# A nineteenth tile for experts' weights, and a pair's sum ahead of the next down products

## The chip, the core and the metric

The kernel runs on one core of a Trainium2 chip. The metric is the time of one execution on the device in microseconds (us). Engines are named as in the profile: PE is TensorE's matmuls, PEld its weight loads, DVE is VectorE, ACT is ScalarE, POOL is GpSimd, SP is SyncE, whose queue issues the DMAs.

## What is computed

256 tokens of width 1024 go through two blocks in float32. The first block mixes tokens (a gated spatial product and a recurrent mixer), then sends every token to 2 of 32 experts and adds their weighted outputs. The second block has two layers of attention, each with a large MLP. The change lies in the experts' stage:

```python
def expert_block(args):
    tok_b, e = args
    xb = xpad[tok_b]
    h = jax.nn.silu(xb @ w_gate[e]) * (xb @ w_up[e])
    return h @ w_down[e]
```

An expert has w_gate and w_up of 1024 x 512 and w_down of 512 x 1024, all float32, 6 MiB together. The 32 experts have 192 MiB, and every one of them is computed.

## The kernel before

**Experts.** A token is given one of 64 slots of its expert. `gather` (L1361) makes the input of four experts at a time, `xg`, by one-hot matrices. For each expert `gate_up` (L1421) multiplies the 64 slots with both matrices, 64 recorded matmuls `gups`, and ScalarE and VectorE make the hidden state `h`. `down_proj` (L1452) calls `hidden_T` (L1444), which transposes `h` on TensorE (`htps`) and lets ScalarE copy it to `hT`; then 16 recorded matmuls `dps` give the outputs. VectorE copies the first 512 columns to the buffer `ysb` of a pair of experts (L1470), ScalarE the other 512 (L1471). `combine` (L1473) multiplies a finished pair with the tokens' weights and adds it into four PSUM banks, 16 recorded matmuls `sums`; the first 8 read what VectorE copied, the other 8 what ScalarE copied. `ysb` has two buffers in the pool `px`.

**The loop** (L1513) is staggered: at step e it asks for gate and up of expert e, then for the down products of expert e-1, and at odd e from 3 on, last, for the sum of the pair (e-3, e-2).

**Weights.** Each matrix is loaded as two tiles of 1 MiB (128 partitions x 8 KB) through SP's queue. The tiles come from three pools: `ring` with 8, `ahead` with 6, `more` with `MORE` = 3, which stands where the mixers' pools stood, and the fourteenth load borrows one buffer of `xg` from `px` once (`BORROW` = 13). So 18 tiles are asked for ahead of the loop, in nine parts of two; afterwards 17 are used in turn. In the order of the loads an expert's gate and up stand ahead of the down matrix of the expert before. A load waits until the last reader of its tile is done. The last 14 tiles but for the borrowed one were used by the loads of the mixers' stage; `px` and `more` start where the pool `split` of the mixers was.

**Order.** The kernel is written with the Tile framework, with `schedule_with_timeline_sim=True`: a planner simulates the program while it is built and fixes each engine's order of instructions. Where the program text names one thing ahead of another, this says which is asked for first, not which is issued first. On the chip the order of each engine is fixed, and semaphores hold an instruction until its inputs are there.

**The branch.** `past_slots` (L1284) holds a slow path for experts with more than 64 tokens. All engines pass the branch at L1287. Its weight tiles `ow` are 2 KB wide, two buffers in the pool `pe`.

Of the kernel before, what the change touches and what calls it, by code (L numbers as in the profile page):

```python
# [13 lines left out]
F32 = mybir.dt.float32  # L14
# [11 lines left out]
P = 128  # L26
T = 256
TX = T + 2
D = 1024
# [5 lines left out]
RING = 8  # L35
SMALL = 4
AHEAD = 6
MORE = 3
BORROW = 13
WAIT = 5  # L40
IDLE = 8
# [3 lines left out]
def block_kernel(ctx: ExitStack, tc: tile.TileContext, A: dict, out: bass.AP):  # L45

    nc = tc.nc
# [73 lines left out]
    loaded = []  # L121
# [529 lines left out]
    with tc.tile_pool(name="pa", bufs=1, reuse_waits="tile") as pa:  # L651
# [129 lines left out]
        for i in range(2):  # L781
            v = f[:, 2 * i : 2 * i + 2, :]
# [18 lines left out]
        for i in range(2):  # L801
            v = sc((P, 2, T), name="qs")
# [290 lines left out]
    with (  # L1093
# [56 lines left out]
        for m in range(2):  # L1150
            v = lgm[:, m].rearrange("p g e -> p (g e)")
# [91 lines left out]
        wg_all, wu_all, wd_all = A["w_gate"][0], A["w_up"][0], A["w_down"][0]  # L1243
        tiles = {}
        rings = [next(source[0]) for _ in range(RING + AHEAD)]
# [4 lines left out]
        def load_next(v, c):  # L1250
            pool = next(rings)
            return load(v, c, pool, "xg" if pool is px else "w")

        source[0] = itertools.repeat(ring)

        def load_expert(e, part):

            if part == "d" and e == NE - 1:
                tiles[e, part] = []
                for i in (0, 512):  # L1260
                    t = next(rings).tile([P, 2048], F32, tag="w", name="w").rearrange("p (k c) -> p k c", c=512)
                    for j in range(2):
                        v = wd_all[e, j * 256 : (j + 1) * 256, i : i + 512].rearrange("(p k) c -> p k c", k=2)
                        loaded.append(nc.sync.dma_start(t[:, 2 * j : 2 * j + 2, :], v))
                    tiles[e, part].append(t)
            elif part == "d":
                tiles[e, part] = [
                    load_next(wd_all[e, i : i + 256, :].rearrange("(p k) c -> p k c", k=2), D) for i in (0, 256)
                ]
            else:  # L1270
                w = wg_all if part == "g" else wu_all
                tiles[e, part] = [
                    load_next(w[e, i : i + 512, :].rearrange("(p k) c -> p k c", k=4), 512) for i in (0, 512)
                ]

        order = []
        for e in range(NE):
            order += [(e, "g"), (e, "u")] + ([(e - 1, "d")] if e else [])
        order.append((NE - 1, "d"))
        nxt = (RING + AHEAD + MORE + 1) // 2  # L1280
        for o in order[:nxt]:
            load_expert(*o)

        def past_slots():  # L1284

            rv = nc.values_load(rint[0:1, 0:1], min_val=0, max_val=T)
            with tc.If(rv > SLOTS):  # L1287
                rb2 = mm(name="rbps")
                spread(r2, rb2[:, 0:T])
                n2T = [sc((P, 2, T), name="n2T") for _ in range(4)]  # L1290
                for k in range(KD):
                    nc.vector.scalar_tensor_tensor(
                        n2T[k // 2][:, k % 2, :],
                        res[:, k, :],
                        col("n2", k, 1),
                        rb2[:, 0:T],
                        op0=ALU.mult,
                        op1=ALU.mult,
                    )
                over = bt("over", (P, 2, NE))  # L1300
                nc.vector.tensor_scalar(over, rank, SLOTS + 0.5, None, op0=ALU.is_ge)
                nc.vector.tensor_tensor(over, over, wt, op=ALU.mult)
                with tc.For_i(0, NE, 1) as ei:
                    wps = mm(name="owps")
                    for m in range(2):
                        nc.tensor.matmul(
                            wps[:, m * P : (m + 1) * P],
                            over[:, m, 0:1].to_broadcast([P, P]),
                            ident,
                            start=True,  # L1310
                            stop=True,
                        )
                    wrow = pe.tile([P, T], F32, tag="hw", name="wrow", bufs=1)
                    nc.vector.tensor_copy(wrow, wps[:, 0:T])

                    def weights(src):
                        w = pe.tile([P, 512], F32, tag="ow", name="ow")
                        w = w.rearrange("p (k c) -> p k c", c=src.shape[2])
                        nc.sync.dma_start(w, src.rearrange("e (k p) c -> p (e k) c", p=P))
                        return w  # L1320

                    for f in range(4):
                        gp = mm((P, 2, T), name="ogp")
                        for s, src in enumerate((wg_all, wu_all)):
                            for k0 in (0, 4):
                                w = weights(src[ds(ei, 1), k0 * P : (k0 + 4) * P, f * P : (f + 1) * P])
                                for k in range(4):
                                    nc.tensor.matmul(
                                        gp[:, s, :],
                                        w[:, k, :],  # L1330
                                        n2T[(k0 + k) // 2][:, k % 2, :],
                                        start=(k0 + k == 0),
                                        stop=(k0 + k == KD - 1),
                                    )
                        o = small.tile([P, T], F32, tag="nf", name="oh", bufs=3)
                        nc.scalar.activation(o, gp[:, 0, :], AF.Silu)
                        nc.vector.tensor_tensor(o, o, gp[:, 1, :], op=ALU.mult)
                        nc.vector.tensor_tensor(o, o, wrow, op=ALU.mult)
                        for c in range(2):
                            w = weights(wd_all[ds(ei, 1), f * P : (f + 1) * P, c * 512 : (c + 1) * 512])  # L1340
                            for pr in range(2):
                                dp = mm((P, 2, T), name="odp")
                                for i in range(2):
                                    k = 2 * pr + i
                                    nc.tensor.matmul(
                                        dp[:, i, :], w[:, 0, k * P : (k + 1) * P], o, start=True, stop=True
                                    )
                                v = res[:, 4 * c + 2 * pr : 4 * c + 2 * pr + 2, :]
                                nc.vector.tensor_tensor(v, v, dp, op=ALU.add)
                    shifted = bt("shifted", (P, 2, NE))  # L1350
                    nc.vector.tensor_copy(shifted[:, :, 0 : NE - 1], over[:, :, 1:NE])
                    nc.vector.tensor_copy(over[:, :, 0 : NE - 1], shifted[:, :, 0 : NE - 1])
# [99 lines left out]
        def down_proj(e, h):  # L1452
            hT = hidden_T(h)
            dt = tiles.pop((e, "d"))
            dps = mm(name="dps")
            for f in range(4):
                j, c = f // 2, f % 2
                for half in range(2):
                    nc.tensor.matmul(  # L1459
                        dps[half * 64 : (half + 1) * 64, :],  # L1460
                        hT[:, c, j * 64 : (j + 1) * 64],
                        dt[f // 2][:, f % 2, half * 512 : (half + 1) * 512],
                        start=(f == 0),
                        stop=(f == 3),
                    )
            e2 = e % 2
            if e2 == 0:
                ysb[e // 2] = px.tile([P, D], F32, tag="ysb", name="ysb")
            t = ysb[e // 2]
            nc.vector.tensor_copy(t[e2 * 64 : e2 * 64 + 64, 0:512], dps[0:64, :])  # L1470
            nc.scalar.copy(t[e2 * 64 : e2 * 64 + 64, 512:1024], dps[64:128, :])  # L1471
# [40 lines left out]
        prev = None  # L1512
        for e in range(NE + 1):  # L1513
            if e < NE:
                while nxt < len(order) and (e, "u") not in tiles:
                    load_expert(*order[nxt])
                    nxt += 1
                h, silu, prod = gate_up(e)
                if e == 0:
                    weigh(0, hot0)  # L1520
                if e % 4 == 2 and e // 4 + 1 < NE // 4:
                    weigh(e // 4 + 1, gather(e // 4 + 1))
            if e:
                if (e - 1, "d") not in tiles:
                    load_expert(*order[nxt])
                    nxt += 1
                if e < NE:
                    down_proj(e - 1, prev)
                if e >= 3 and e % 2 == 1:
                    combine((e - 3) // 2)  # L1530
            prev = h
            if e == 8:
                with ExitStack() as es:
# [832 lines left out]
```

## Time and profile before

| | us |
|---|---|
| median of 3 runs | 1307.55 (1306.39 to 1308.12) |
| the profiled execution | 1305.86 |
| its span, first to last instruction | 1304.2 |
| PE busy | 1260.6 (97%) |
| DVE busy | 651.8 (50%) |
| ACT busy | 511.8 (39%) |

The granted TensorE clock is 0.99 of full speed over the span. The experts' stage goes from about 147 us (first gate matmul) to about 606 us (last sum). The profile's matmuls are pipelined, so the time between two starts says more than one matmul's duration. A float32 matmul is recorded as two.

### The profile page before, as it was taken

What the parts mean: (1) busy time and instruction counts of PE and PEld (TensorE: products, weight loads), DVE (VectorE), ACT (ScalarE), POOL (GpSimd) and SP (SyncE); (2) the same over time, 40 slices, a digit from 0 to 9 for tenths busy, and PEclk for the clock granted to TensorE, in tenths of its full rate; (3) what the DMA queues carried; (4) which work ended last, traced back from release to release, by engine and by line L of the source; (5) the groups of instructions that cost most, each with busy time, mean ns of one, the idle gap of its engine ahead of it and who ended that gap; (6) DMA issues with size and microseconds to landing.
All of it is one profiled execution on the core that took longest, in us unless ns stands there. A gap on an engine that the chain in (4) does not pass through costs nothing.

```text
span 1304.2 us, 22821 instructions
## 1 busy us (share of the span) xinstructions
PE 1260.6 (97%) x9471; PEld 998.6 (77%) x9471; DVE 651.8 (50%) x1268; ACT 511.8 (39%) x918; POOL 65.2 (5%) x92
## 2 busy tenths in 40 slices
PE   8999899999999999999998999999999999999998
PEld 7779565665555556556885679999997879999998
DVE  6765310130101111004776777698667787655554
ACT  7743211111101111113455656544544564654644
POOL 1010000000000000000410000000001120000000
PEclk9999899999999999998998999999999999999999
DMA  7997799999999999998554845599677532555510
GB/s 252 363 411 300 289 421 420 421 421 421 421 420 420 421 421 421 420 415 305 167 195 153 328 164 199 182 353 338 249 272 271 178 130 77 180 172 187 194 66 33
DMA packets 99157, 373.98 MB, mean 287 GB/s; under 512 B 10649, under 2 KB 14442, under 8 KB 74730
## 3 DMA queue, kind: packets, MB, share of 16 engines
q1 hardware_dynamic: 99050, 372.49, 75.1%
q8 instruction: 76, 1.25, 0.4%
q14 instruction: 31, 0.25, 0.1%
HBM read 371.41 MB, written 1.05 MB: 286 GB/s over the span
## 4 chain that ended last, share of the span: by engine, by line
PE 74%; issue 11%; DVE 2%; ACT 1%; POOL 0%; DVEq 0%; ACTq 0%; POOLq 0%
PE hp L448 14%; PE mlp L491 14%; PE gups L1429 13%; PE dps L1459 6%; PE dps L469 5%; PE sums L1477 3%; PE gps L1383 2%; PE oearly L584 2%; PE qp L469 2%; PE olate L491 2%; PE adaps L187 1%; PE kv L469 1%; PE opair L2119 1%; PE kcv L469 1%; PE ptps L2110 1%
## 5 line engine op out<-in xcount | busy, mean ns | idle before, releaser
L152 DVE TENSOR_TENSOR wlo<-w,whi 128x1024 fp32r<-128x1024 f32 (+1 forms) x222 | 269.7, 1218 | 160.9 <-ACT whi L151 158.6
L151 ACT CAST whi<-w 128x1024 fp32r<-128x1024 f32 (+1 forms) x222 | 230.5, 1043 | 251.0 <-PE hp L448 105.6
L1429 PE MATMUL gups<-w,xg 128*64 128x256 f32 x2048 | 236.2, 384 | 3.5 <-PEq L1287 3.5
L1429 PEld LDWEIGHTS gups<-w,xg 128*64 128x64 f32 x2048 | 145.6, 138 | 91.6 <-issue 22.6
L491 PE MATMUL mlp<-hid,whi 128*128 128x256 f32 x1024 | 184.0, 282 | 0.0
L491 PEld LDWEIGHTS mlp<-hid,whi 128*128 128x128 f32 x1024 | 157.2, 188 | 0.4 <-issue 0.4
L491 PE MATMUL mlp<-hid,wlo 128*128 128x256 f32 x512 | 144.8, 283 | 0.0
L448 PE MATMUL hp<-hT_lo,whi 128*128 128x258 f32 x512 | 144.0, 282 | 0.0
L448 PE MATMUL hp<-hT_hi,whi 128*128 128x258 f32 x512 | 143.7, 283 | 0.0
L448 PE MATMUL hp<-hT_hi,wlo 128*128 128x258 f32 x512 | 142.5, 282 | 0.0
L1441 DVE TENSOR_TENSOR h<-h,gups 128x256 f32<-128x256 f32 x32 | 13.5, 421 | 235.8 <-ACT h L1440 235.8
L1459 PE MATMUL dps<-w,hT 128*64 128x512 f32 x496 | 112.7, 596 | 5.1 <-ACT hT L1449 5.1
L491 PEld LDWEIGHTS mlp<-hid,wlo 128*128 128x128 f32 x512 | 96.4, 188 | 1.6 <-issue 1.6
L448 PEld LDWEIGHTS hp<-hT_lo,whi 128*128 128x128 f32 x512 | 96.7, 189 | 0.0
L448 PEld LDWEIGHTS hp<-hT_hi,whi 128*128 128x128 f32 x512 | 96.2, 188 | 0.0
L448 PEld LDWEIGHTS hp<-hT_hi,wlo 128*128 128x128 f32 x512 | 95.9, 189 | 0.0
L1440 ACT ACTIVATE h<-gups 128x256 f32<-128x256 f32 x32 | 12.3, 385 | 183.6 <-PE gups L1429 183.6
L1459 PEld LDWEIGHTS dps<-w,hT 128*64 128x64 f32 x496 | 34.1, 137 | 64.3 <-issue 53.0
L1470 DVE COPY ysb<-dps 64x512 f32<-64x512 f32 x31 | 21.2, 683 | 107.0 <-PE dps L1459 107.0
L1471 ACT COPY ysb<-dps 64x512 f32<-64x512 f32 x31 | 18.0, 582 | 139.0 <-DVE ysb L1470 139.0
L1477 PE MATMUL sums<-sw,ysb 128*128 128x256 f32 x256 | 61.3, 385 | 6.3 <-DVE ysb L1470 6.3
L1477 PEld LDWEIGHTS sums<-sw,ysb 128*128 128x128 f32 x256 | 46.4, 190 | 20.0 <-DVE ysb L1470 13.3
(539 smaller groups left out, 2014.5 us busy)
## 6 DMA issues: line engine op xcount, KB each, us to landing
w<-in_w_gate_dram SPq DMA_DIRECT2D x64, 1024.0 KB
w<-in_w_up_dram SPq DMA_DIRECT2D x64, 1024.0 KB
w<-in_w_down_dram SPq DMA_DIRECT2D x62, 1024.0 KB
w<-in_w_ada_dram SPq DMA_DIRECT2D x48, 1024.0 KB
w<-in_w_mlp_in_dram SPq DMA_DIRECT2D x32, 1024.0 KB
w<-in_w_mlp_out_dram SPq DMA_DIRECT2D x32, 1024.0 KB
w<-in_diff_w_in_dram SPq DMA_DIRECT2D x12, 1024.0 KB
w<-in_w_in_dram SPq DMA_DIRECT2D x10, 1024.0 KB
```

The lines of the kernel that those rows point to most:

```text
L151: nc.scalar.copy(hi, v)
L152: nc.vector.tensor_tensor(lo, v, hi.bitcast(F32), op=ALU.subtract)
L448: nc.tensor.matmul(outs[h], a[:, kk, h * P : (h + 1) * P], b[:, k, :], start=(k == 0 and i == 0), stop=(k == KD - 1 and i == 2),)
L469: nc.tensor.matmul(outs[m], b[:, k, m * P : (m + 1) * P], a[:, kk, :], start=(k == 0 and i == 0), stop=(k == KD - 1 and i == 2),)
L491: nc.tensor.matmul(outs[dc // 2][:, dc % 2, :], a[:, 0, dc * P : (dc + 1) * P], b[:, a0 + kk, :], start=(first and kk == 0 and i == 0 and ...
L584: nc.tensor.matmul(banks[h // 2][:, h % 2, :], a[:, kk, h * P : (h + 1) * P], b[:, k, :], start=(k == 0 and i == 0 and h % 2 == 0), stop=( ...
L1383: nc.tensor.matmul(ps[:, j, :], part[:, m, k * P : (k + 1) * P], hot[:, m].rearrange("p e s -> p (e s)"), start=(n == 0), stop=(n == 3),)
L1429: nc.tensor.matmul(ps[j * 64 : (j + 1) * 64, s * 256 : (s + 1) * 256], xg[:, k, s0 : s0 + SLOTS], w[k // 4][:, k % 4, j * 256 : (j + 1) * ...
L1459: nc.tensor.matmul(dps[half * 64 : (half + 1) * 64, :], hT[:, c, j * 64 : (j + 1) * 64], dt[f // 2][:, f % 2, half * 512 : (half + 1) * 51 ...
L1470: nc.vector.tensor_copy(t[e2 * 64 : e2 * 64 + 64, 0:512], dps[0:64, :])
L1471: nc.scalar.copy(t[e2 * 64 : e2 * 64 + 64, 512:1024], dps[64:128, :])
L1477: nc.tensor.matmul(sums[k // 2][:, k % 2, :], t[:, k * P : (k + 1) * P], sw, start=(pr == 0 and k % 2 == 0), stop=(after is not None and k ...
```

## The change

`MORE` becomes 4, so that 19 tiles are asked for ahead of the loop and 18 are used in turn. The room of 8 KB per partition comes from two places: `ysb` has one buffer instead of two (4 KB), and the branch's tiles `ow` (2 x 2 KB) use that buffer. As the number of tiles ahead is odd, loads are asked for tile by tile instead of in pairs (`load_expert` has an argument `i`, and `load_until` loads until both tiles of a part are there). With one output buffer, the sum of a pair must be asked for ahead of the next pair's first output, so `combine` moves ahead of `down_proj`.

```diff
-MORE = 3
+MORE = 4
...
-        nxt = (RING + AHEAD + MORE + 1) // 2
-        for o in order[:nxt]:
-            load_expert(*o)
+        order = iter([(*o, i) for o in order for i in range(2)])
+
+        def load_until(*o):
+            while len(tiles.get(o, ())) < 2:
+                load_expert(*next(order))
+
+        for _ in range(RING + AHEAD + MORE + 1):
+            load_expert(*next(order))
...
-                        w = pe.tile([P, 512], F32, tag="ow", name="ow")
+                        w = px.tile([P, D], F32, tag="ysb", name="ow", bufs=1)[:, 0:512]
...
-                ysb[e // 2] = px.tile([P, D], F32, tag="ysb", name="ysb")
+                ysb[e // 2] = px.tile([P, D], F32, tag="ysb", name="ysb", bufs=1)
...
-                while nxt < len(order) and (e, "u") not in tiles:
-                    load_expert(*order[nxt])
-                    nxt += 1
+                load_until(e, "u")
...
-                if (e - 1, "d") not in tiles:
-                    load_expert(*order[nxt])
-                    nxt += 1
+                load_until(e - 1, "d")
+                if e >= 3 and e % 2 == 1:
+                    combine((e - 3) // 2)
                 if e < NE:
                     down_proj(e - 1, prev)
-                if e >= 3 and e % 2 == 1:
-                    combine((e - 3) // 2)
```

## Rows read from the trace of the kernel before

**Rows 1.** The page: what the DMAs moved, in 40 equal slices of the span.
```profile
GB/s 252 363 411 300 289 421 420 421 421 421 421 420 420 421 421 421 420 415 305 167 195 153 328 164 199 182 353 338 249 272 271 178 130 77 180 172 187 194 66 33
```
**Rows 2.** By stretch: us, then PE, PEld, DVE, ACT, POOL; PE's clock, DMA share, GB/s.
```profile
160.00:200.00 40.00, 39.08 (x288) 23.89 (x286) 6.58 (x14) 5.54 (x13) 1.04 (x1) 1.00 1.01 421
```
**Rows 3.** Waits of PE, 146 to 600 us: total, times, longest.
```profile
PE sums L1477 <- DVE ysb L1470: 6.3, 8, 0.8
PE dps L1459 <- ACT hT L1449: 5.1, 10, 0.5
```
**Rows 4.** Waits of the weight loads, the same stretch: the largest that names a DMA.
```profile
PEld gups L1429 <- DMA w<-in_w_up_dram: 3.0, 10, 0.3
```
**Rows 5.** PE in order of time, experts 10 to 12: start, us, what.
```profile
280.38 7.08 PE L1429 MATMUL gups<-w,xg 128*64 128x256 f32 x64
...
292.63 3.65 PE L1459 MATMUL dps<-w,hT 128*64 128x512 f32 x16 [0.52 <-ACT hT L1449]
296.11 7.08 PE L1429 MATMUL gups<-w,xg 128*64 128x256 f32 x64
303.12 0.44 PE L1447 MATMUL htps<-ident,h 128*128 128x128 f32 x2
303.39 3.62 PE L1477 MATMUL sums<-sw,ysb 128*128 128x256 f32 x16
306.94 3.65 PE L1459 MATMUL dps<-w,hT 128*64 128x512 f32 x16
...
317.44 0.44 PE L1447 MATMUL htps<-ident,h 128*128 128x128 f32 x2
318.39 3.65 PE L1459 MATMUL dps<-w,hT 128*64 128x512 f32 x16 [0.52 <-ACT hT L1449]
```
**Rows 6.** PE in order of time, experts 13 and 14.
```profile
321.87 1.90 PE L1429 MATMUL gups<-w,xg 128*64 128x256 f32 x16
...
333.75 3.65 PE L1459 MATMUL dps<-w,hT 128*64 128x512 f32 x16
337.23 1.90 PE L1429 MATMUL gups<-w,xg 128*64 128x256 f32 x16
...
350.51 3.65 PE L1459 MATMUL dps<-w,hT 128*64 128x512 f32 x16 [0.52 <-ACT hT L1449]
```
**Rows 7.** PE in order of time, experts 15 to 17.
```profile
354.00 1.90 PE L1429 MATMUL gups<-w,xg 128*64 128x256 f32 x16
355.82 0.44 PE L1447 MATMUL htps<-ident,h 128*128 128x128 f32 x2
356.10 3.62 PE L1477 MATMUL sums<-sw,ysb 128*128 128x256 f32 x16
...
364.88 3.60 PE L1459 MATMUL dps<-w,hT 128*64 128x512 f32 x16
...
375.74 3.60 PE L1459 MATMUL dps<-w,hT 128*64 128x512 f32 x16
380.13 1.99 PE L1477 MATMUL sums<-sw,ysb 128*128 128x256 f32 x8 [0.79 <-DVE ysb L1470]
...
391.26 1.03 PE L1459 MATMUL dps<-w,hT 128*64 128x512 f32 x4
```
**Rows 8.** The last expert's products on PE, and SP's first loads behind the experts.
```profile
596.49 2.76 PE L1496 MATMUL dps<-w,hT 128*64 128x256 f32 x24
...
578.48 11.98 SPq L131 DMA_DIRECT2D w<-in_nsa_w_in_dram  x4
```
**Rows 9.** Ahead of the loop: PE, SP's issues, and the DMA share (columns as rows 2).
```profile
128.83 0.29 PE L491 MATMUL olate<-hT_hi,wlo 128*128 128x256 f32 x1
...
128.32 0.33 SPq L131 DMA_DIRECT2D w<-in_w_up_dram  x1
...
150.98 2.79 SPq L131 DMA_DIRECT2D w<-in_w_up_dram  x2
...
143.00:151.00 8.00, 4.54 (x23) 2.78 (x24) 2.29 (x9) 2.03 (x3) 1.04 (x1) 0.65 0.20 76
```

More of the change, by code (lines that the diff above doesn't have):

```diff
@@ L1254, in block_kernel, with load_expert @@
         source[0] = itertools.repeat(ring)
-        def load_expert(e, part):
+        def load_expert(e, part, i):
             if part == "d" and e == NE - 1:
[L1259 to L1265, printed above, removed]
+                t = next(rings).tile([P, 2048], F32, tag="w", name="w").rearrange("p (k c) -> p k c", c=512)
+                for j in range(2):
+                    v = wd_all[e, j * 256 : (j + 1) * 256, i * 512 : (i + 1) * 512].rearrange("(p k) c -> p k c", k=2)
+                    loaded.append(nc.sync.dma_start(t[:, 2 * j : 2 * j + 2, :], v))
             elif part == "d":
-                tiles[e, part] = [
-                    load_next(wd_all[e, i : i + 256, :].rearrange("(p k) c -> p k c", k=2), D) for i in (0, 256)
-                ]
+                t = load_next(wd_all[e, i * 256 : (i + 1) * 256, :].rearrange("(p k) c -> p k c", k=2), D)
             else:
                 w = wg_all if part == "g" else wu_all
-                tiles[e, part] = [
-                    load_next(w[e, i : i + 512, :].rearrange("(p k) c -> p k c", k=4), 512) for i in (0, 512)
-                ]
+                t = load_next(w[e, i * 512 : (i + 1) * 512, :].rearrange("(p k) c -> p k c", k=4), 512)
+            tiles.setdefault((e, part), []).append(t)
         order = []
```

## The prediction

> **What bounds the kernel now.** I read the page first, then the stage of the experts, which the change touches. TensorE is busy for 97% of the span by its table of engines, and from the fifth to the eighteenth of the 40 slices the DMA engines are full as well, at about 421 GB/s [rows 1]. So two things could set the pace of the 32 experts: TensorE, or the 192 weight tiles of 1 MiB. The table by stretches shows both at their limit at once: PE 39.08 of 40 us, DMA share 1.01 [rows 2].
>
> The waits decide. In 146 to 600 us TensorE's idle time before matmuls has, beside the one branch, two causes: 6.3 us for a pair's output that VectorE had not yet copied (8 times 0.79), 5.1 us for the transposed hidden state that ScalarE had not yet copied (10 times 0.51) [rows 3]. Weights are in the list of the weight loads only, three rows of which this is the largest: 10 waits, 3.0 us together, none over 0.3 [rows 4]. The lead can be worked out too. After the branch the queue starts again at 150.98 with the tile that waited for the first one to be read [rows 9]. From there 174 tiles of 1.0486 MB at 0.421 MB/us take 433 us, so the last lands near 587 (2 us added from issue to flow, an estimate from the end of idle DMA in [rows 9]). Its products start at 596.49, its second half a little over a microsecond later [rows 8]: some 10 us of lead at the tightest place. TensorE sets the pace, and within it the order of its own instructions, which was written at build time by a planner that simulated the kernel.
>
> That order comes in two forms. Early ("closed"), an odd expert's 64 gate/up matmuls run in one piece, then the transpose, the pair's 16 sums, and the down products: 303.12, 303.39, 306.94. An even expert has no sums; its down products start 0.95 us after its transpose (317.44 to 318.39), 0.52 us of it idle [rows 5]. From expert 13 on ("open") the planner believed that weights come late and broke the 64 up into groups of 16 with other work between [rows 6]; from expert 17 on the first 8 sums stand directly behind the down products that they read, and TensorE stalls 0.79 us for the copy [rows 7].
>
> **The change, part by part.** The sum is made on the profiled execution, 1305.86 us (span 1304.2), which lies 1.69 us under the median of 1307.55; at the end I add 1.69.
>
> *A nineteenth tile.* It is loaded in time that was free: from 143 to 151 us the DMA share is 0.20 [rows 9]. Every later load then starts one tile earlier, 1.0486/0.421 = 2.49 us. For TensorE's waits this is worth 0, since no weight is waited for; what hides it is the 10 us of lead, and if that cover were absent the gain would be the whole 2.49. The loads behind the experts (attention's) come earlier or wait for ring tiles that the last experts now hold; they were issued from 578.48 [rows 8] and the last of those tiles is read by about 600, so I take 0 here. Issuing tile by tile instead of in pairs changes no DMA and adds none.
>
> *What the planner makes of it.* It believes in late weights from expert 13's second gate tile on, number 77 in the order (an expert's gate starts at 6e - 2, counted from 0), where the first break stands [rows 6]. Its lead of 17 tiles lasted until there; 18 should last 77 x 18/17, to about number 82, which is expert 14's first. So expert 13 closes. From its first gate/up to its down products it took 333.75 - 321.87 = 11.88 us; expert 11, closed, took 306.94 - 296.11 = 10.83 [rows 5, 6]. Expert 14 took 350.51 - 337.23 = 13.28, its like, expert 10, 292.63 - 280.38 = 12.25 [rows 5, 6]: between 0 and -1.03, I take half, -0.5, as its first tile is just at the border. Expert 15 took 364.88 - 354.00 = 10.88; closed in the new way it would take 11.51 (below): 0 to +0.63, I take +0.2. From down products to down products, experts 15 and 17 took 14.37 and 15.52 [rows 6, 7]: if expert 17 gets 15's form, -1.15; between 0 and that I take -0.4, as this form needs weights early by more than one shift gives.
>
> *The sum ahead of the next down products.* Before, the program asked for the transpose, the down products, then the sum. The planner followed that order wherever both were ready: at expert 15 the transpose goes first at 355.82, the sums at 356.10 [rows 7], and the sums filled the wait for the hidden state's copy. Now the sum is asked for ahead of the transpose. In the closed form both are ready when the gate/up matmuls end, so I expect 64 gate/up, 16 sums, transpose, stall, down products. The stall that even experts show then stands in odd ones too: 0.95 instead of 303.39 - 303.12 = 0.27, or +0.68 each. Nothing else can fill it: at the even experts nothing does. Closed odd experts with a sum are 3, 5, 7, 9, 11: 5 x 0.68 = +3.4. Bounds: 0 if the planner keeps the transpose ahead, +3.4 if it swaps all. I take the swap, by the row at 355.82. Expert 13 becomes 10.83 + 0.68 = 11.51 against 11.88: -0.37. In the open form the second 8 sums and the transpose only change places ahead of 48 gate/up matmuls, which cover the copy: 0.
>
> *One output buffer instead of two.* The first down copy of a pair (VectorE, then ScalarE) now waits for the sums of the pair before. Behind it on VectorE stands the next expert's product, and TensorE's next transpose waits for that. But the sums stand ahead of those down products on TensorE, which is in order, so the wait is over before the copy is ready: 0. If the sums stood behind the down products it would cost up to a group of sums, 3.55 us a pair [rows 5].
>
> *The branch's tiles* share that buffer. The branch isn't taken in the profile (nothing of its lines is busy), so 0.
>
> *The rooms move by 4 KB.* The third to sixth weight tiles now start 4 KB lower and the first of them reaches into the last buffer of the split pool, whose last reader is the olate product at 128.83 [rows 9]. That tile (half of expert 0's up) is read only after the first gate tile, so after 150.98, and a load issued at 128.32 already waits for that stage's end [rows 9]. So 0 by the idle DMA time that follows; the other end is rival (d).
>
> Sum: +3.4 - 0.37 - 0.5 + 0.2 - 0.4 = +2.3. Bounds with the swap: 3.4 - 0.37 - 1.03 - 1.15 = +0.85, and 3.4 - 0.37 + 0.63 = +3.7. Profiled 1308.2, median **1309.9** (own range 1308.4 to 1311.3).
>
> **Rivals.**
> (a) *The planner leaves the transpose ahead.* Then +3.4 goes and expert 13 gains its 1.05: -1.05 - 0.5 - 0.4 = -1.95 with no gain on 15. For it: its priorities aren't in the trace. Against: the row at 355.82. Median 1305.6.
> (b) *Open experts lose the stall behind the copy.* With weights believed earlier, gate/up would stand ahead of the sums as at expert 15, in all eight odd experts: 8 x -1.15 = -9.2 with the rest as forecast without expert 17's -0.4: -6.5. Median 1301.0. For it: one tile turned 17's form at 15. Against: in that stretch the planned TensorE waits for every tile, and a lead of one tile is used up after an expert.
> (c) *The DMA is the bound*, and the tile's 2.49 us come off whole: median 1305.1. For it: share 1.01 [rows 2]. Against: [rows 4].
> The Trainium skill, Perfetto Trace Analysis, section Roofline, would read this stage so: it puts a single core's practical ceiling near 120% of 358 GB/s. The measured 421 GB/s are 118% of that, so by this rule the stage is at the memory's ceiling and case (c) holds; the waits of TensorE speak against it.
> (d) *Slower: the planner gets nothing from the tile and still swaps.* Its loads may be tied to something other than the number of tiles: the room of the third tile is free only behind the product at 128.83, SP's queue is in order, and whatever is placed behind that load stands with it, so that the queue resumes at 150.98 with 18 tiles as before [rows 9]. Then experts 13 to 17 stay as they are, and only the swaps are paid: 1305.86 + 5 x 0.68 = 1309.3, median 1311.0. It decides where expert 13 still opens. Should still fewer tiles be in by 151 us, the lead of 10 us covers four of them (4 x 2.49), so this adds at most the fifth and sixth, 5 us, which I leave outside. For it: [rows 9]. Against: 8 us of idle DMA follow, room for three tiles.
>
> **How the numbers follow.** Chances: forecast 0.43, (a) 0.15, (b) 0.14, (c) 0.08, (d) 0.20. About 0.2%, or 2.6 us, is what a measurement of this kernel can tell from no change: 1304.9 to 1310.2. The forecast's own range lies across its upper edge: same 0.25, slower 0.18. (a) is same 0.09, faster 0.06; (b) faster; (c) same 0.04, faster 0.04; (d) slower. Together faster 0.24, same 0.38, slower 0.38. The range leaves out the larger part of (b), and adds one more tile's 2.49 us above (d): 1302.5 to 1314, with some 0.15 left out.
>
> **What would show it.** Right: in the closed stretch the sums start right behind 64 gate/up matmuls and each odd expert's down products show about 0.5 us of wait for the hidden state's copy, 15 such waits instead of 10; 19 expert tiles issued before 151 us; the 8 waits for the pair's copy still 7 or 8; TensorE's waits for weights still under 0.3 us. Wrong: the transpose still ahead of the sums; or the waits for the pair's copy gone; or expert 13 opened as before.

## The result: slower, and by four times the forecast

Before 1306.39 us (median of 5 runs, 1302.75 to 1308.12), after 1316.01 us (5 runs, 1313.16 to 1317.08): ratio 1.0073, 95% interval 1.0058 to 1.0088, so +9.6 us (+7.6 to +11.5) where the forecast was +2.3. It lies above the range. The profiled execution of the changed kernel took 1316.01 us (span 1314.3, granted clock 0.987), that of before 1305.86 (1304.2, 0.990).

The 40 slices of the changed kernel's page answer to [rows 1]. The experts' stage, slices 6 to 17, runs at 420 to 422 GB/s as before. The two slices ahead of it do not: 193 and 365, before 300 and 289. The loads were put off and then came in a burst.

```profile
GB/s 251 368 411 193 365 421 421 420 422 421 421 420 421 421 420 421 420 413 276 153 205 152 328 160 199 184 353 335 250 273 254 178 129 70 180 175 187 192 65 33
```

TensorE's waits from 146 to 600 us answer to [rows 3] (total, times, longest). The copy's waits went from 10 to 15, as forecast, and the eight waits of the sums stayed. New is a wait of 3.5 us put down to "issue": TensorE ran nothing, and the profile shows nothing that it waited for. (PEq is TensorE's sequencer; its wait at L1286 is the branch.)

```profile
PE dps L1458 <- ACT hT L1448: 6.9, 15, 0.5
PE sums L1476 <- DVE ysb L1469: 6.3, 8, 0.8
PE gups L1428 <- issue: 3.5, 1, 3.5
PE gups L1428 <- PEq L1286: 2.6, 1, 2.6
```

Where that wait stands is seen in order of time, TensorE first, then the stretch of [rows 9] with the same columns, then SP's loads:

```profile
143.10 0.27 PE L1235 MATMUL rps<-ident,rmx 128*1 128x128 f32 x1
145.98 1.91 PE L1428 MATMUL gups<-w,xg 128*64 128x256 f32 x14 [2.60 <-PEq L1286]
151.35 7.46 PE L1428 MATMUL gups<-w,xg 128*64 128x256 f32 x50 [3.46 <-issue]
158.74 0.66 PE L1411 MATMUL wps<-ident,hw 128*128 128x128 f32 x4
...
143.00:151.00 8.00, 2.29 (x18) 1.30 (x17) 2.21 (x9) 1.95 (x3) 1.04 (x1) 1.00 1.01 414
...
120.23 0.33 SPq L131 DMA_DIRECT2D w<-in_w_down_dram  x1
129.07 0.80 SPq L131 DMA_DIRECT2D w<-in_w_up_dram  x2
129.93 1.11 SPq L131 DMA_DIRECT2D w<-in_w_gate_dram  x2
...
136.54 19.84 SPq L131 DMA_DIRECT2D w<-in_w_up_dram  x2
156.48 0.96 SPq L131 DMA_DIRECT2D w<-in_w_down_dram  x2
```

SP stood from 120 to 129.07 us behind one load, whose lowered room the olate product still held; it and the two behind it had gone at 112.38 to 113.85 before. Then nine went out, and the DMAs, idle at a share of 0.20 before [rows 9], were full (1.01) from 143 to 151 us. In that stretch every engine passes the branch on the slot count. TensorE ran 14 gate matmuls behind it and stood from 147.89 to 151.35. SP issued its first load behind the branch at 156.04 us, before at 150.98.

What the DMA queues carried then points to why (queue, kind: packets, MB, share), first from 145.5 to 148.4 us, then from 148.4 to 151.4:

```profile
q1 hardware_dynamic: 183, 1.25, 103.6%
...
q1 hardware_dynamic: 156, 1.16, 96.1%
q8 instruction: 1, 0.02, 2.7%
q14 instruction: 2, 0.02, 1.4%
```

Up to 148.4 us nothing but weights; the instruction packets, which bring code, came at 148.59 to 148.66. In the kernel before they came at 146.20 to 147.16. The largest was in at 149.96, and TensorE went on at 151.35.

Behind the pause the changed kernel lost once more, by its clock. These are the stretches from 150 to 156 us of the changed kernel, then from 147 to 153 us of the kernel before (columns as [rows 2]; the clock stands ahead of the DMA share):

```profile
150.00:153.00 3.00, 1.65 (x9) 1.32 (x10) 0.00 (x0) 0.00 (x0) 0.00 (x0) 0.74 0.99 412
153.00:156.00 3.00, 3.00 (x22) 2.58 (x20) 0.00 (x0) 0.00 (x0) 0.00 (x0) 0.69 0.13 49
...
147.00:150.00 3.00, 3.00 (x15) 1.83 (x17) 0.51 (x2) 0.00 (x0) 0.00 (x0) 0.50 0.03 5
150.00:153.00 3.00, 3.00 (x19) 1.99 (x18) 0.00 (x0) 0.00 (x0) 0.00 (x0) 0.62 0.30 60
```

In the closed experts the swap stands as forecast. This is expert 11, and answers to [rows 5]; expert 13 behind it is still open:

```profile
300.14 7.08 PE L1428 MATMUL gups<-w,xg 128*64 128x256 f32 x64
307.15 3.72 PE L1476 MATMUL sums<-sw,ysb 128*128 128x256 f32 x16
310.70 0.38 PE L1446 MATMUL htps<-ident,h 128*128 128x128 f32 x2
311.55 3.65 PE L1458 MATMUL dps<-w,hT 128*64 128x512 f32 x16 [0.46 <-ACT hT L1448]
315.03 7.08 PE L1428 MATMUL gups<-w,xg 128*64 128x256 f32 x64
...
326.42 1.90 PE L1428 MATMUL gups<-w,xg 128*64 128x256 f32 x16
328.25 0.44 PE L1446 MATMUL htps<-ident,h 128*128 128x128 f32 x2
```

From gate to gate the expert takes 315.03 - 300.14 = 14.89 us, before 310.43 - 296.11 = 14.32.

How late TensorE's instructions stand against before, profile against profile: first W product (`wps`, the first matmuls behind expert 0's gate and up; 158.74 against 156.79) +1.95; start of expert 12 +4.61; first products of the last expert +4.29; the norm's broadcast (`rbps`) behind the experts +5.64; end +10.16. So 2.66 us came in the closed experts, and nearly six behind the last one. How much of the first and last of these belongs to the change and how much to one execution, a pair of profiles cannot say; the experiments had to.

### The profile page after: what moved, and what is told of

Read it like the earlier page. It is cut to its first block, busy times and chain, and to the rows that moved or that the text cites. A ratio compares the mean times of both kernels' runs of the same rounds, so it can differ in the third digit from the quotient of the medians.

```text
span 1314.3 us, 22791 instructions
## 1 busy us (share of the span) xinstructions
PE 1263.3 (96%) x9471; PEld 1001.5 (76%) x9471; DVE 652.9 (50%) x1268; ACT 511.9 (39%) x918; POOL 65.7 (5%) x92
## 3 DMA queue, kind: packets, MB, share of 16 engines
HBM read 371.41 MB, written 1.05 MB: 283 GB/s over the span
## 4 chain that ended last, share of the span: by engine, by line
PE 74%; issue 11%; DVE 1%; ACT 1%; DMA 0%; POOL 0%; DVEq 0%; POOLq 0%; ACTq 0%
PE hp L448 14%; PE mlp L491 14%; PE gups L1428 12%; PE dps L1458 6%; PE dps L469 5%; PE sums L1476 3%; PE gps L1382 2%; PE oearly L584 2%; PE qp L469 2%; PE olate L491 2%; PE adaps L187 1%; PE kv L469 1%; PE opair L2114 1%; PE kcv L469 1%; PE ptps L2105 1%
```

## The experiments

Twelve runs, of which e8 is the changed kernel again; each time is against runs of the kernel before on the same chip. In us, the ratio less 1 (with its interval) times 1305.

**e1, the sum ahead, alone**, on the kernel before:

```diff
+                if e >= 3 and e % 2 == 1:
+                    combine((e - 3) // 2)
                 if e < NE:
                     down_proj(e - 1, prev)
-                if e >= 3 and e % 2 == 1:
-                    combine((e - 3) // 2)
```

> The kernel before with one edit: the pair's sum is asked for ahead of the next down products (18 tiles, two output buffers, rooms as before). Theory of parts: the time of the change is a sum of a start of the experts' stage that is 1.95 us late (rooms), five closed odd experts that lose 0.52 us each (the sum ahead), and 5.9 us behind the experts that belong to neither. Then this kernel shows the second part alone: first gate/up stage as before (W product at about 156.8 us), 16 sums ahead of the transpose in the closed odd experts, +2.2 to +3.1 us in the time, and no further loss behind the experts. Rival, the sum is the whole: +9.6 us. Rival, whatever is late at the experts' end costs again behind them: +2.6 there and 5 to 6 behind, together about +8 us.

Measured: 1309.03 us against 1304.55, ratio 1.0030 (1.0018 to 1.0043), +3.9 (+2.3 to +5.6). The part is a little above its bracket, far from the +9.6 of the first rival; in its profile 3.0 us are lost from the first W product to the last expert. With 18 tiles, expert 13 is now closed, and has the wait too:

```profile
323.30 7.08 PE L1429 MATMUL gups<-w,xg 128*64 128x256 f32 x64
330.31 3.72 PE L1477 MATMUL sums<-sw,ysb 128*128 128x256 f32 x16
333.87 0.38 PE L1447 MATMUL htps<-ident,h 128*128 128x128 f32 x2
334.76 3.65 PE L1459 MATMUL dps<-w,hT 128*64 128x512 f32 x16 [0.52 <-ACT hT L1449]
```

**e2, the changed kernel with the transpose first:**

```diff
+                hT = hidden_T(prev) if e < NE else None
                 if e >= 3 and e % 2 == 1:
                     combine((e - 3) // 2)
                 if e < NE:
-                    down_proj(e - 1, prev)
+                    down_proj(e - 1, hT)
...
```

> The changed kernel with the transpose of the hidden state asked for ahead of the pair's sum (order: transpose, sum, down products; 19 tiles, one output buffer). Theory of parts: the five losses of 0.52 us go, the late start of 1.95 us and the loss behind the experts stay: +7 us against before, some tenths more because one more expert (12) is planned with late weights. Rival, the sum is the whole: 0 us. If the one output buffer costs something of its own, the first down copy of a pair waits on VectorE for the sums: waits of several tenths that the kernel before doesn't have.

Measured: 1311.69, ratio 1.0056 (1.0036 to 1.0076), +7.3. As expected: without the sum ahead, most of the loss is still there. Expert 12 is the first open one.

**e3, the held room used late**, on the changed kernel: the weight tile that lies lowest gets a pool of its own and is the fifteenth to be loaded.

```diff
-        rings = rings[:2] + [more] * MORE + rings[2:]
+        rings = rings[:2] + [more] * (MORE - 1) + rings[2:]
+        rings = rings[:BORROW] + [late] + rings[BORROW:]
...
```

> The changed kernel, but the weight tile whose room reaches into the split pool's last buffer is used fifteenth instead of third, so that the loads of the others don't stand behind the olate product. Theory: SP's queue then issues its loads at 112 to 120 us as before, the nineteenth tile lands near 148.4 us instead of 151, TensorE's pause behind its first gate matmuls ends by as much earlier, and the experts start 0 to 1 us late instead of 1.95; expert 13 is planned closed. Time +7 to +8 us against before (2 us less than the changed kernel). Rival, the pause behind the branch has nothing to do with the loads: it ends at 151.35 us as in the changed kernel, +9.6 us.

Measured: 1310.45, ratio 1.0041 (1.0026 to 1.0055), +5.3, more of a gain than expected. TensorE doesn't stop: 64 gate/up matmuls run through from 146.16, first W product at 155.38, instruction packets at 146.42 to 146.59.

**e4, the queue held, with nothing else of the change**, on the kernel before:

```diff
-BORROW = 13
+BORROW = 2
...
+                if 3 < len(seen) <= 6:
+                    es.enter_context(tc.issue_after(third[0].ins))
...
```

> The kernel before with its 18 tiles, but the room that is held by the olate product (the px tile) is used for the third tile, and the next three loads are kept behind it, so that SP's queue stands until 129 us and then issues eight loads in a burst, as in the changed kernel. Nothing else of the change is in it. Theory: the weights then still move at 146 to 148.5 us, TensorE gets its code behind the branch late and stands until about 149 us after some 14 gate matmuls, the experts start about 1 to 2 us late, and expert 12 is planned open: +1 to +2.5 us. Rival, the loads have nothing to do with the pause: no pause, 0 us (0.5 with expert 12).

Measured: 1309.58, ratio 1.0035 (1.0024 to 1.0045), +4.6, above the expected +1 to +2.5. The pause is there and longer than expected; packets at 149.74 to 150.12. Here the clock fell ahead of the pause, and the 50 matmuls behind it ran at 1.00:

```profile
147.33 3.54 PE L1440 MATMUL gups<-w,xg 128*64 128x256 f32 x14 [3.14 <-PEq L1298]
152.78 5.77 PE L1440 MATMUL gups<-w,xg 128*64 128x256 f32 x50 [1.92 <-issue]
158.49 0.66 PE L1423 MATMUL wps<-ident,hw 128*128 128x128 f32 x4
```

**e5, both costs out** (the edits of e2 and e3 together):

> The changed kernel with both costs taken out: transpose ahead of the sum (as e2) and the held room used fifteenth (as e3). What is left of the change is the nineteenth tile, one output buffer and the branch's shared tiles; TensorE's order of the experts is that of the kernel before. Theory of the sum (sum ahead about +3.4 us, held queue about +4.6, from e1 to e4): 9.6 - 8 leaves +1 to +2 us. Rival, the tile's 2.49 us of DMA time come off: -2.5 us. Rival, neither tile nor buffer matters: 0 us. First W product at about 155 us, no pause behind the 14th gate matmul.

Measured: 1306.73 against 1305.97, ratio 1.0012 (1.0000 to 1.0024), +1.6 (0 to +3.1). What is left of the change gains nothing. TensorE's order of the experts is that of before, expert 13 the first open one: the tile moves nothing in the planner.

**e6, 16 tiles on the kernel before** (`MORE = 1`, the two tiles' room left empty):

> The kernel before with 16 tiles instead of 18 (the two tiles' room is left empty, all addresses as before). The weights are then in by about 141 us. Theory, code behind the branch comes through the DMA engines and queues behind weights: its packets, at 146.2 to 147.2 us before, come 0.5 to 2 us earlier, TensorE doesn't pause behind its 14th gate matmul, first W product at 155 us or earlier. And as no weight is waited for with 18 tiles (10 us of lead), 16 leave 5 us and cost nothing but expert 12 planned open: -1.5 to +0.5 us. Rival, a tile of lead is worth its 2.49 us: +5 us.

Measured: 1307.03, ratio 1.0012 (1.0003 to 1.0021), +1.6, above its bracket of -1.5 to +0.5. Two tiles fewer don't cost their 5 us; expert 12 is the first open one, as expected. The first half was a miss: packets at 146.24 to 147.27 as before and first W product at 156.92, but the weights, expected in by 141 us, ran on until 145 as before, so whether more quiet brings the code earlier was not tried.

**e7, the queue held, 16 tiles** (e4's edit on e6, with one load kept behind the third instead of three), so that the burst ends ahead of the branch:

> The kernel of e4 (queue held until 129 us by the third tile) with 16 tiles instead of 18, so that the burst is short and the weights are in by about 144 us. Theory, the cost of e4 is that weights still move when the branch's code is fetched: no pause behind the 14th gate matmul, first W product at about 155 us (e4: 158.49), 0 to +1 us against before. Rival, holding the queue costs by itself: +4.6 us as e4.

Measured: 1307.32, ratio 1.0008 (0.9998 to 1.0019), +1.0 (-0.3 to +2.5). Holding costs next to nothing if the loads are done in time:

```profile
146.96 8.81 PE L1442 MATMUL gups<-w,xg 128*64 128x256 f32 x64 [2.74 <-PEq L1300]
155.70 0.66 PE L1425 MATMUL wps<-ident,hw 128*128 128x128 f32 x4
```

**e8, the changed kernel again:**

> The changed kernel once more, on the chip of e5 to e7, to see what of its trace comes back. Theory: +8 to +10 us; instruction packets behind the branch at 148 us or later, TensorE's pause behind the 14th gate matmul until 151 us, first W product between 156.9 and 158.8 us. If that was one execution's accident, no pause, and +4 to +6 us.

Measured: 1314.77 against 1305.97, ratio 1.0071 (1.0058 to 1.0084), +9.3. Packets at 149.06 to 149.32, TensorE stands until 151.95, first W product at 159.27, half a us later than expected. It was no accident.

**e9, the sums behind a gate matmul**, on the kernel before. The eight waits of the sums [rows 3] stand in both versions; this edit goes for them:

```diff
-                    combine((e - 3) // 2)
+                    with tc.issue_after(gate[0].ins):
+                        combine((e - 3) // 2)
...
```

> The kernel before (18 tiles, two output buffers) with one edit: a pair's sums may not be placed ahead of the next expert's first gate matmul. In the eight odd experts that are planned with late weights, TensorE's order becomes 16 gate, transpose, 16 sums, 48 gate/up, down products, the form of expert 15, which is rival (b) of the prediction made by hand. Theory: the eight waits of the sums for the pair's copy (6.3 us) go, at up to 1.15 us each: -6 to -9 us. Rival, TensorE then runs into the loads (10 us of lead): waits for weights appear late in the stage, and only -2 to -4 us are left. Rival, the copies are waited for elsewhere: 0 us.

Measured: 1298.35 against 1306.02, ratio 0.9943 (0.9929 to 0.9957), -7.4: faster than both kernels. The sums' waits are gone; at the end of the stage TensorE meets the loads, for 2.1 us in four waits:

```profile
PE dps L1462 <- ACT hT L1452: 5.1, 10, 0.5
PE gups L1430 <- PEq L1287: 2.6, 1, 2.6
PE dps L1462 <- DMA w<-in_w_down_dram: 1.1, 2, 0.6
PE ssps L328 <- ACT sq L314: 0.7, 1, 0.7
PE gups L1430 <- DMA w<-in_w_gate_dram: 0.6, 1, 0.6
PE gups L1430 <- DMA w<-in_w_up_dram: 0.4, 1, 0.4
```

**e10, the same edit on e5** (19 tiles):

> The kernel of e5 (19 tiles, held room used late, transpose ahead of the sum, one output buffer) with the edit of e9. TensorE's order of the experts is that of e9. If loads limit e9 near the end of the stage, the nineteenth tile is worth up to its 2.49 us here: e9 less 1 to 2.5 us. If they don't, the tile is worth nothing again and this is e9 plus the 0 to 1.6 us of e5: -5 to -8 us against before.

Measured: 1298.75, ratio 0.9945 (0.9930 to 0.9959), -7.2. In the experts' stage the tile now does what it was added for: of the waits for weights one of 0.2 us is left, and from the first W product to the last expert's last products this kernel gains 9.7 us on before, e9 6.7. In the time nothing of it is seen: the two can't be told apart, and 1.5 us of it go behind the experts in the profile, 1.05 of them at the norm's root (last section).

**e11, traffic alone**: e7 with two loads that nobody reads, ahead of the branch.

```diff
+        for t in pads:
+            v = wg_all[0, 0:512, :].rearrange("(p k) c -> p k c", k=4)
+            with tc.issue_after(loaded[-1].ins):
+                loaded.append(nc.sync.dma_start(t.rearrange("p (k c) -> p k c", c=512), v))
...
```

> The kernel of e7 (16 tiles, queue held until 129 us) with two more loads of 1 MB each in front of the branch, into the room that e7 leaves empty; nobody reads them. They are traffic alone, and bring the weights' end back to about 149 us as in e4. Theory, the branch's code waits for the weights that are under way: its packets come at 149 us or later (e7: 146.99 to 147.15), TensorE stops behind the 14th gate matmul, first W product at 157 to 159 us (e7: 155.70), and the time is 2 to 4 us over e7's +1.0 us (some tenths of it because the planner, which counts the two loads, opens expert 10 instead of 12). Rival, what cost e4 was its tiles and not the traffic: packets at 147 us, first W product at 155.7 us, +1 to +1.5 us.

Measured: 1313.22 against 1305.50, ratio 1.0059 (1.0040 to 1.0077), +7.7, more than expected. Packets at 148.79 to 149.00, and the pause is back:

```profile
146.07 3.08 PE L1446 MATMUL gups<-w,xg 128*64 128x256 f32 x14 [2.61 <-PEq L1304]
151.53 8.41 PE L1446 MATMUL gups<-w,xg 128*64 128x256 f32 x50 [2.38 <-issue]
159.87 0.66 PE L1429 MATMUL wps<-ident,hw 128*128 128x128 f32 x4
```

The first W product is 4.2 us later than in e7; the clock had fallen to 0.50 by 147 us and stayed there to 156, so part of this is the clock. The planner opened expert 10, at a cost of some 2.5 us more in the profile (shift against before +3.07 at the W product, +5.54 at expert 16).

**e12, GpSimd's root first**, on e10:

```diff
-    hold(dve=mean)
+    spare = small.tile([P, 2], F32, name="spare", tag="spare")
+    hold(dve=nc.vector.tensor_copy(spare, means[:, 1, :]))
```

> The kernel of e10 with one small copy more on VectorE (128x2) between the variance of the last norm and the split of the next weight, so that this split starts behind GpSimd's first root and not 0.03 to 0.04 us ahead of it as in the four profiles with 19 tiles. Theory: the root then takes 0.70 us instead of 1.75, TensorE waits 1.3 us instead of 2.3 at that place, and the time is about 1 us below e10 (-8 us against before). Rival, the root's length has another cause (the program's length, the loads under way): 1.75 us again, and e10's time.

Measured: 1300.57 against 1305.50, ratio 0.9961 (0.9949 to 0.9974), -5.1. In the trace it does what was expected: TensorE waits 1.3 us for the root instead of 2.3. In the time it isn't there; the median is not below e10's. The profiled execution, 1294.57 us, was the fastest of twelve, so its trace is not that of the median. The granted clock over the span was 0.992 in the two fastest and 0.986 to 0.990 in the ten others; what lowered it stays open.

## Why the prediction was wrong

- *The nineteenth tile, 0 for TensorE's waits:* right. e5 gained nothing, 16 tiles cost no 5 us (e6). Rival (c) is out here; only when TensorE was made faster did it meet the loads (e9: 2.1 us, with the tile 0.2, e10). But "loaded in time that was free" was the error next door: the time was free of weights, not of use. (The prediction has the DMAs full from the fifth slice on; the fifth reads 289 GB/s and the sixth 421 [rows 1], and nothing hangs on it.)
- *The rooms, 0:* this is the step that failed. The prediction saw the third tile's room behind the olate product and SP's queue in order behind it, and priced the burst at nothing "by the idle DMA time that follows". Through that idle stretch came the code behind the branch. Its price is e4 less e7, 4.6 - 1.0 = 3.6 us, some 2 us either way by the two intervals; e11 brings it back with traffic alone. Over all profiles: where the weights are in by about 147 us, in e3 but for a remainder (before, e1, e3, e5, e6, e7, e9, e10, e12) the first W product stands at 154.1 to 156.9 us, mean 155.5; where they aren't (after, e2, e4, e8, e11) at 156.9 to 159.9, mean 158.7: 3.2 us. The +1.95 between the first two profiles is too low, because that of before had a slow start: TensorE waited 3.5 us at the branch, not 2.6, and ran at a granted clock of 0.50 (1.2 of 2.4 GHz) from 147 to 150 us. The changed kernel was at 1.00 until its pause ended and at 0.50 from 152 to 154 us: its 50 matmuls behind the pause took 7.39 us start to start, 5.71 in e4. So the late code cost it 3.46 us of standing and, if the fall of the clock behind the pause belongs to it, 1.7 more.
- *Rival (d), place right, price wrong:* it named this room, this product and this queue, and then had SP resume at 150.98 "with 18 tiles as before". All 19 went out, SP resumed at 156.04, and the cost was in TensorE's code, which (d) did not look at.
- *The swap, +3.4:* right in place, order and count (five; waits 10 to 15). Each cost 0.53 in the profile (2.66 in five) and not 0.68, as the down products begin 0.85 us behind the transpose and not 0.95. By e1, with a sixth expert closed, +3.9 (+2.3 to +5.6).
- *What the planner makes of the tile, -1.07 in all:* wrong. The lead in its books does not go by the number of tiles alone: with 16 tiles expert 12 is the first open one (e6), with 18 and with 19 alone expert 13 (before, e5); with the queue held it is 12 (e2, e4), with the sum ahead 14 (e1). In the change the last two cancel, which looked like rival (d)'s "gets nothing". Measured from expert 12 to the last: 4.29 - 4.61 = -0.32.
- *One output buffer, the branch's tiles, 0:* right as far as e5 resolves it, +1.6 (0 to +3.1) with all else that is left. No wait of VectorE's or TensorE's for the buffer appeared.
- *Rival (a)* is out by the rows of expert 11, *(b)* by the eight waits that stayed; its 8 x -1.15 was a fair price, as e9 got -7.4 by making that order by hand.
- *Left out of the forecast: what is behind the experts.* Nearly 6 us of the first pair of profiles. Two pieces come back in the 19-tile kernels: 1.05 us at the norm's root (below; not in e12), and 0.5 to 0.9 us at the very end. There all seven profiles with 19 tiles fetch one more 8 KB instruction packet (queue 14) behind the last copy of the output and end 4.6 to 5.0 us behind that copy's start, the seven with 18 or 16 fetch none there and end at 4.0 to 4.1. Together they are about as much as e5's +1.6; why the program's end lies so was not tried. Some is the granted clock: in the 20 us around the start of the attention's projections (before from 980, after from 987) it is 1.00 before and 0.91 after, and the shift grows by 1.63 there, from 6.29 to 7.92; e1, e4, e6, e7 and e8 show that step too, e2, e3, e5 and e9 to e12 don't. It was not tried what sets it. Over whole runs, the mean granted clock was 0.9892 in e8 and 0.9915 in the 29 runs of before on its chip, among which a thousandth more goes with 0.8 us less: an estimate of some 2 of the 9.3 us that go with the clock, the pause's share included.

The sum by experiments: sum ahead 3.9, queue held 4.6, the rest (e5) 1.6, together 10.1 where 9.6 and 9.3 were measured. Against the forecast, the miss of 7.3 us is the room (3.6 to 4.6), what e1 lies above the swap with its planner terms (3.9 - 2.3 = 1.6), and e5's 1.6. The parts account for the change within their intervals; how each part's loss spreads over the stages behind the experts stays open.

## What to carry to other kernels

An idle stretch of DMA is free only if nothing else is fetched through it: where engines pass a branch, have the loads done by then, or the code behind it may come late, as it did here by 2 to 3 us. When a room moves, look which load of the queue it delays and where the delayed ones land together. And a wait that both versions share (the sums' eight) may be worth more than what the change moves.

## What the hardware showed that was not expected

*Code behind a branch comes late while bulk loads are under way.* The instruction packets (16 KB on queue 8, twice 8 KB on queue 14) came at 145.7 to 147.3 us in the nine profiles in which the weights were in or nearly, and at 148.6 to 150.1 in the five in which weights still moved in bulk. TensorE ran exactly 14 gate matmuls ahead of the pause in each of the seven profiles with one (e1 and e5 have short ones, 0.96 and 0.80 us), and in each it went on 1.2 to 1.5 us behind the end of the 16 KB packet, wherever that lay between 147.2 and 151.3 us. So it stood for its code. That code did not wait for the last weight: in the changed kernel the weights ran on at a share of 0.93 or more until 153 us. The Trainium skill states that a taken branch to a page that is not yet held needs a DMA fetch before execution goes on (Runtime: NRT & Kernel Launch, section Instruction fetch mechanics); these traces agree, as the slow path is passed over here. The Trainium skill also says that a DMA engine takes turns between queues packet by packet (DMA: Bandwidth & Descriptors, section Queues, rings and completion order); by that rule the code should not wait for megabytes, and here it came 2 to 3 us late. When the fetch was asked for, no trace shows, so whether the request or the transfer was late stays open.

*A tenth of a us decides over one us.* GpSimd's first root takes 0.70 us where it begins 0.06 us ahead of VectorE's split and 1.75 where the split began 0.03 us earlier. These are GpSimd's rows in e10 and, last, in e12, where the split was put 0.16 us behind the root:

```profile
597.26 1.75 POOL L1796 TENSOR_TENSOR roots<-means,mhalf 128x2 f32<-128x2 f32 x1 [138.32 <-DVE means L1793]
...
597.23 0.70 POOL L1796 TENSOR_TENSOR roots<-means,mhalf 128x2 f32<-128x2 f32 x1 [137.93 <-DVE means L1793]
```

All kernels with 18 tiles show 0.70; those with 19 show 1.75 (1.74 once) but for e12, and those with 16 show 1.62, with the split 0.16 us ahead. The Trainium skill has it as a port pair that VectorE and GpSimd share and that goes whole to whoever starts first (SBUF — State Buffer, section Who interferes with whom); e12 agrees on GpSimd's side. The split takes 1.23 us in either order, so no wait of VectorE's is seen.
